# A norm's first tile made in two parts, token rows turned one tile later, 58 early U blocks and eight output buffers

## The chip, the cores and the metric

The kernel runs on one core of a Trainium2 chip, as one program. The metric is the device time of one execution in microseconds (us). The kernel before takes 4063.26 us as the median of three executions (4061.71 to 4071.17).

TensorE multiplies matrices and writes the products to PSUM; VectorE and ScalarE work element by element; GpSimd (POOL) and SyncE (SP) mostly issue transfers between the chip's memory and SBUF. Each engine runs its own instructions in a fixed order and waits for the others by semaphores.

## The reference

Two request groups, a context of 128 tokens and a latent grid of 512 tokens, go through the same weights; the kernel carries all 640 tokens side by side as columns. There are two layers. The first mixes tokens by a gated short convolution, the second by a bidirectional state-space scan (SSD). Behind each stands a PEER mixer, in which each token picks 8 x 16 of 16384 single-neuron experts:

```python
hn = rmsnorm(x, norm_mix_g[i]) * (1 + scl_a) + sh_a      # and again ahead of peer, with scl_f, sh_f
# short_conv_mixer
bg, cg, xv = jnp.split(h @ w_in, 3, axis=-1)
return (bg * dwconv3(cg * xv, conv_w, grid)) @ w_out
# peer: scores, the 16 best keys of each half, the 16 best pairs, softmax gates g, experts idx
act = jnp.einsum('td,thkd->thk', tb, u[ib])
out = jnp.einsum('thk,thkd->td', jax.nn.gelu(act, approximate=False) * gb, v[ib])
# end of the trunk
return rmsnorm(x, norm_f_g), states
```

All of it is in 32-bit floats.

## The kernel before

**Layout.** `x` lies in SBUF as 8 feature tiles of 128 partitions (features) x 640 columns (tokens, 512 latent and 128 context). A product at full accuracy is three matmuls of rounded parts: high x high, high x low, low x high (`mm3`, L128 to L130). So each operand is split: ScalarE writes the high part (L92 for weights, L123 for activations), VectorE subtracts it to get the low part (L101, L124). For weights these are `wr` (raw), `wh`, `wl`, and `ur`, `uh`, `ul` for the expert keys U.

**The norm** (`norm`) goes through the 8 feature tiles: VectorE multiplies a tile of `x` by the reciprocal root `rs` (L330), ScalarE applies scale and shift to the latent and the context columns separately (L332, 512 and 128 columns), then the tile is split into its high and low part (`chi`, `clo` in the conv layer, `shi`, `slo` in the SSD layer, `hnh`, `hnl` ahead of the experts). Ahead of the experts a function `token_rows` is called for each tile (as `keep`): POOL copies a few tokens' columns out of it into `some` (L774), TensorE transposes them (`pss`, `psx`, L776), and after four tiles ScalarE copies the rows out (`hrow`, L778).

**The conv layer** follows its norm with 24 weights: `cg`, `xv` and `bg` in turn for each of 8 output tiles. In the first output tile (`rows=(j == 0)`) the products go by feature tile, so that they can follow the norm. Transposes of `silurow` (`srow`, L436) stand near by. Products of the norm's output have 320 columns (half of 640).

**The experts.** Of the 512 latent tokens, 464 are done densely: for each of 128 blocks of 128 experts, TensorE multiplies the block of U by the tokens (`pact`, 24 matmuls of 464 columns), ScalarE applies Gelu into a ring of five buffers `ga` (L511), VectorE multiplies by the gates `gt` (L577) to get `h`, and TensorE multiplies `h` by the block of V (`acc` and `rot`, 24 matmuls more). The other 176 tokens' worth of work (48 latent tokens, and the context in 128 parts) is done by gathers: an indirect transfer of 128 rows of U and V side by side (`uv`, 1 MB, L592, issued by POOL, three buffers), a dot product (L599) and a weighted sum (L609) on VectorE. The first `NSP` blocks of U are multiplied early, while top-k and the gates run on VectorE; their `ga` is stored to memory by POOL (`adram`, L513) and read back by SP when its turn comes (`load_act`, L570). Then one loop goes over the 128 blocks of V. In its first part (block number + `LAG` below `NSP`) it has only V's products, 24 matmuls a turn; in the second part U's block three turns ahead stands beside them, 48 matmuls a turn. `GATHER` gives the gathers per turn in the two parts. VectorE adds `rot` into `sacc` (L647 the first time, L649 later).

**Order.** Most of the program is put in order by a scheduler that uses a cost model; the last part of the early blocks and the loop stand in the order in which the code is written (`manual_schedule`). Just ahead of the loop the code issues two gathers and the first `gt` on POOL's queue, then the remaining early blocks (`fill`), then three `load_act`. SP's and POOL's queues each go in order: a transfer whose buffer isn't free holds all that are behind it.

**The end.** `final` multiplies the 8 tiles by `rs` and the last norm's weight into `fo` (L218, three buffers) and stores each (`yT`, L220).

Of the kernel before, what the change touches and what calls it, by code (L numbers as in the profile page):

```python
# [9 lines left out]
F32 = mybir.dt.float32  # L10
# [5 lines left out]
AF = mybir.ActivationFunctionType  # L16
# [5 lines left out]
P = 128  # L22
NL = 512
NT = 640
# [5 lines left out]
KT = 8  # L30
D = 1024
HALF = 320
EPS = 1e-6
NBLK = 128
NSP = 56
LAG = 3
GA = 4
TB = 16
# [1 line left out]
SW = 64  # L40
CH = 5
FILL_Q = (0, 8500)
GATHER = (0.60, 1.98)
START = 4
MORE = (1, 1, 0, 4)
ADA_C = 16
# [7 lines left out]
SEGS = ((0, NL, 0), (NL, NT, 1))  # L54
# [62 lines left out]
class K:  # L117
# [28 lines left out]
    def run(s):  # L146
        nc, A = s.nc, s.A
        with ExitStack() as ctx:
# [4 lines left out]
            s.gdram = dram.tile([NBLK // GA, P, ND // SG, GA, SG], F32, name="gdram")  # L153
            s.adram = dram.tile([NSP, P, ND], F32, name="adram")
            s.sdram = dram.tile([1, 2, D], F32, name="sdram")
# [56 lines left out]
    def final(s):  # L212
        nc = s.nc
        with ExitStack() as ctx:
            tp = s.pool(ctx, "ftmp")
            for k in range(KT):
                o = tp.tile([P, NT], F32, name="fo", bufs=3)
                nc.vector.scalar_tensor_tensor(o, s.x[:, k, :], s.sv("nff", KT)[:, k:k + 1], s.rs,  # L218
                                               op0=ALU.mult, op1=ALU.mult)
                nc.sync.dma_start(s.A["yT"][:, k, :], o)  # L220
# [104 lines left out]
    def norm(s, i, j, hi, lo, tp, keep=None, ks=range(KT)):  # L325

        nc = s.nc
        for k in ks:
            t = tp.tile([P, NT], F32, name="nt", bufs=3)
            nc.vector.tensor_mul(t, s.x[:, k, :], s.rs)  # L330
            for a, b, c in SEGS:
                nc.scalar.activation(t[:, a:b], t[:, a:b], AF.Identity, bias=s.mod[i][:, 24 * j + k, c:c + 1],  # L332
                                     scale=s.gs[i][:, j, k, c:c + 1])
            s.split(hi[:, k, :], lo[:, k, :], t)
            if keep is not None:
                keep(k, t)

    def proj(s, w, hi, lo, out, rows=False):

# [144 lines left out]
    def peer(s, i):  # L484
        nc, A = s.nc, s.A
        with ExitStack() as ctx:
# [15 lines left out]
            def u_blocks():  # L502
                for a in range(NBLK):
# [7 lines left out]
                    nc.scalar.activation(g, pa, AF.Gelu)  # L511
                    if a < NSP:
                        nc.gpsimd.dma_start(s.adram[a], g)  # L513
# [7 lines left out]
            def fill(ns, steps=0):  # L521

                state["owe"] += ns
                while (steps > 0 or ns and state["owe"] > 0) and state["n"] < NSP * KT:
                    t = next(ub)
                    if not steps:
                        state["owe"] -= t
                    steps -= 1 if steps else 0
                    state["n"] += 1
                U.split(state["n"] // KT + 2)  # L530
# [8 lines left out]
            with ExitStack() as mc:  # L539
# [27 lines left out]
                def load_act(a):  # L567
                    if a < NSP:
                        t = ring.tile([P, ND], F32, name="ga")
                        nc.sync.dma_start(t, s.adram[a])  # L570
                        ga[a] = t
# [60 lines left out]
                state["owe"] = 0  # L632
                fill(0, NSP * KT - state["n"] - KT)
                for a in range(LAG):
# [16 lines left out]
                for a in range(NBLK - 2):  # L651
                    V.high(a + 2)
                    if a + LAG >= NSP:
                        U.high(a + LAG + 2)
# [21 lines left out]

                    credit += GATHER[0] if a + LAG < NSP else GATHER[1]
                    due, before = 0, slot
# [793 lines left out]
```

## Time and profile before

| what | us |
|---|---|
| runs | 4061.71, 4063.26, 4071.17 |
| profiled execution | 4057.71 |
| its span | 4056.0 |
| TensorE busy | 3915.4 (97%) |
| VectorE busy | 3394.0 (84%) |
| ScalarE busy | 1663.2 (41%) |
| POOL busy | 514.9 (13%) |
| granted TensorE clock, mean | 0.987 |

From the span's start the stages are: ada modulation, conv norm and conv layer to 277 us; the norm ahead of layer 0's experts to 304; top-k, gates and early blocks to 787; the loop to 1822; the SSD layer, whose norm stands at 1836, to 2491; the second layer's experts with their norm (2494), early blocks (to 2990) and loop (from 2999) to 4020; the last norm to 4056. "Idle before" an instruction is the time in which its engine had nothing to run, and the arrow says what ended it. The granted clock is the share of TensorE's full speed.

### The profile page before, as it was taken

How to read it: one execution, taken by the hardware profiler on the slowest of the kernel's cores; microseconds unless marked ns; L12 is line 12 of the kernel's file. 1: busy time of each engine (PE TensorE's matmuls, PEld its weight loads, DVE VectorE, ACT ScalarE, POOL GpSimd, SP SyncE). 2: the span in 40 equal slices, each digit the busy share in tenths (PEclk: the TensorE clock that was granted, in tenths of full speed). 3: DMA queues.
4: the chain of work that ended last, by engine and by line, in shares of the span. 5: the costliest groups of instructions: out<-in, count | busy, mean ns of one | idle time of the engine just before them, and what ended most of it. 6: DMA issues, size and time to landing. Idle time of an engine off the chain costs nothing.

```text
span 4056.0 us, 59421 instructions
## 1 busy us (share of the span) xinstructions
PE 3915.4 (97%) x22237; PEld 3548.9 (87%) x22237; DVE 3394.0 (84%) x6512; ACT 1663.2 (41%) x3120; POOL 514.9 (13%) x695
## 2 busy tenths in 40 slices
PE   8999999899999999999999999999989999999998
PEld 6989988788888888888899998998878888888887
DVE  8978988588878888887999856998768888888887
ACT  5233344433334333336555644334433333343333
POOL 0010000011112212211110101000011111121211
PEclk9999999999999999999999999999999999999999
DMA  6643258988889989973333234226888898998995
GB/s 228 218 154 121 83 171 248 287 318 312 329 311 338 341 325 333 339 274 126 114 102 119 88 114 173 83 99 192 251 296 314 316 334 316 337 335 329 333 333 222
DMA packets 337451, 979.15 MB, mean 241 GB/s; under 512 B 39371, under 2 KB 174795, under 8 KB 291081
## 3 DMA queue, kind: packets, MB, share of 16 engines
q1 hardware_dynamic: 146922, 508.73, 35.7%
q0 software_dynamic: 64000, 398.47, 26.4%
q10 hardware_dynamic: 126240, 68.16, 5.9%
q8 instruction: 174, 2.85, 0.3%
q14 instruction: 115, 0.94, 0.1%
HBM read 867.00 MB, written 108.14 MB: 240 GB/s over the span
## 4 chain that ended last, share of the span: by engine, by line
issue 41%; PE 29%; DVE 15%; POOL 9%; DMA 4%; ACT 2%; POOLq 0%; SPq 0%; ACTq 0%; DVEq 0%
POOL uv L592 9%; PE pact L128 2%; DMA ur<-uT 2%; PE pact L130 2%; PE pj L128 2%; PE pact L129 2%; PE pj L129 2%; PE pj L130 2%; DVE ul L101 2%; DVE wl L101 1%; PE bank L128 1%; PE bank L129 1%; PE bank L130 1%; PE bank L1189 1%; PE pg L999 1%
## 5 line engine op out<-in xcount | busy, mean ns | idle before, releaser
L128 PE MATMUL pact<-hnh,uh 128*128 128x464 f32 x2048 | 774.2, 378 | 1.0 <-DVE xt L623 1.0
L130 PE MATMUL pact<-hnh,ul 128*128 128x464 f32 x2048 | 768.3, 375 | 0.0
L129 PE MATMUL pact<-hnl,uh 128*128 128x464 f32 x2048 | 766.6, 374 | 0.0
L592 POOL DMA_INDIRECT uv<-uv,cidx x352 | 362.2, 1029 | 1698.6 <-DVE cacc L609 1567.2
L128 PE MATMUL acc<-h,wh 128*128 128x464 f32 x1536 | 575.4, 375 | 0.0
L130 PE MATMUL acc<-h,wl 128*128 128x464 f32 x1536 | 575.3, 375 | 0.0
L129 PE MATMUL acc<-h,wh 128*128 128x464 f32 x1536 | 573.1, 373 | 0.0
L92 ACT ACTIVATE wh<-wr 128x1024 fp32r<-128x1024 f32 x385 | 404.9, 1052 | 377.8 <-DMA wr<-uv 92.5
L599 DVE SCALAR_TENSOR_TENSOR uv<-uv,hrow 128x1024 f32<-128x1024 f32 x352 | 430.1, 1222 | 128.5 <-DMA uv<-uv,cidx 125.3
L101 DVE TENSOR_TENSOR wl<-wr,wh 128x1024 fp32r<-128x1024 f32 x385 | 469.8, 1220 | 54.7 <-ACT wh L92 54.4
L609 DVE SCALAR_TENSOR_TENSOR cacc<-uv,dg,cacc 128x1024 f32<-128x1024 f32 x346 | 443.4, 1282 | 0.0
L130 PEld LDWEIGHTS pact<-hnh,ul 128*128 128x128 f32 x2048 | 386.4, 189 | 45.5 <-DVE ul L101 0.3
L128 PEld LDWEIGHTS pact<-hnh,uh 128*128 128x128 f32 x2048 | 387.2, 189 | 44.6 <-DVE xt L623 1.3
L129 PEld LDWEIGHTS pact<-hnl,uh 128*128 128x128 f32 x2048 | 387.2, 189 | 44.3
L511 ACT ACTIVATE ga<-pact 128x464 f32<-128x464 f32 x256 | 141.8, 554 | 582.6 <-PE pact L130 578.9
L101 DVE TENSOR_TENSOR ul<-ur,uh 128x1024 fp32r<-128x1024 f32 x256 | 312.1, 1220 | 56.0 <-ACT uh L92 55.9
L92 ACT ACTIVATE uh<-ur 128x1024 fp32r<-128x1024 f32 x256 | 268.3, 1050 | 184.7 <-PE pact L129 81.0
L129 PEld LDWEIGHTS acc<-h,wh 128*128 128x128 f32 x1536 | 291.0, 189 | 36.0
L130 PEld LDWEIGHTS acc<-h,wl 128*128 128x128 f32 x1536 | 290.0, 189 | 34.9
L128 PEld LDWEIGHTS acc<-h,wh 128*128 128x128 f32 x1536 | 290.7, 189 | 33.8
L601 ACT ACTIVATE dg<-dg 128x1 f32<-128x1 f32 x352 | 70.6, 200 | 540.4 <-DVE uv L599 540.0
L586 DVE TENSOR_TENSOR h<-h,h 128x464 fp32r<-128x464 f32 x256 | 163.8, 640 | 127.7 <-PE rot L129 123.8
(346 smaller groups left out, 7978.1 us busy)
## 6 DMA issues: line engine op xcount, KB each, us to landing
ur<-uT SPq DMA_DIRECT2D x256, 512.0 KB
wr<-uv SPq DMA_DIRECT2D x256, 512.0 KB
gt<-gdram SPq DMA_DIRECT2D x62, 928.0 KB
gdram<-st ACTq DMA_DIRECT2D x28, 2048.0 KB
mw<-ada_wT SPq DMA_DIRECT2D x80, 512.0 KB
adram<-ga POOLq DMA_DIRECT2D x112, 232.0 KB, 4.1
ga<-adram SPq DMA_DIRECT2D x112, 232.0 KB
wr<-ssd_w SPq DMA_DIRECT2D x48, 512.0 KB
```

Source lines behind the costliest of these rows:

```text
L92: s.K.nc.scalar.activation(hi.rearrange("p a b -> p (a b)"), s.raw[s.nh], AF.Copy)
L101: s.K.nc.vector.tensor_sub(lo.rearrange("p a b -> p (a b)"), s.raw.pop(s.ns), hi.rearrange("p a b -> p (a b)").bitcast(F32))
L128: mm(out, wh, mh, start=start, stop=False)
L129: mm(out, wh, ml, start=False, stop=False)
L130: mm(out, wl, mh, start=False, stop=stop)
L511: nc.scalar.activation(g, pa, AF.Gelu)
L586: nc.vector.tensor_sub(h2, h, h1.bitcast(F32))
L592: nc.gpsimd.indirect_dma_start(out=t[:], out_offset=None, in_=A["uv"].rearrange("l e d -> (l e) d"), in_offset=bass.IndirectOffsetOnAxis(a ...
L599: nc.vector.scalar_tensor_tensor(UV[n][:, :D], UV[n][:, :D], 1.0, rows[-1], op0=ALU.mult, op1=ALU.mult, accum_out=dg[:, n:n + 1])
L601: nc.scalar.activation(dg[:, n:n + 1], dg[:, n:n + 1], AF.Gelu)
L609: nc.vector.scalar_tensor_tensor(cacc, t[:, D:], dg[:, n:n + 1], cacc, op0=ALU.mult, op1=ALU.add)
L999: nc.tensor.matmul(g[:, q, :], oh[:, t + q, :], o1[:, t + q, :], start=True, stop=False)
```

## The change

The constant `NSP` goes from 56 to 58 and the gather rates from (0.60, 1.98) to (0.62, 2.0). `fo` gets eight buffers instead of three. In `norm`, the first feature tile is multiplied, modulated and split in two parts, columns 0 to 320 and 320 to 640; the others in one part as before. `keep` (the token rows) of tile k is called after tile k+1 is made, and that of the last tile at the end. All four norms that use this function are touched: conv, SSD, and the two ahead of the experts.

```diff
-NSP = 56
+NSP = 58
...
-GATHER = (0.60, 1.98)
+GATHER = (0.62, 2.0)
...
-                o = tp.tile([P, NT], F32, name="fo", bufs=3)
+                o = tp.tile([P, NT], F32, name="fo", bufs=KT)
...
+        late = None
         for k in ks:
             t = tp.tile([P, NT], F32, name="nt", bufs=3)
-            nc.vector.tensor_mul(t, s.x[:, k, :], s.rs)
-            for a, b, c in SEGS:
-                nc.scalar.activation(t[:, a:b], t[:, a:b], AF.Identity, bias=s.mod[i][:, 24 * j + k, c:c + 1],
-                                     scale=s.gs[i][:, j, k, c:c + 1])
-            s.split(hi[:, k, :], lo[:, k, :], t)
+
+            for p, q in ((0, HALF), (HALF, NT)) if k == 0 else ((0, NT),):
+                nc.vector.tensor_mul(t[:, p:q], s.x[:, k, p:q], s.rs[:, p:q])
+                for a, b, c in SEGS:
+                    a, b = max(a, p), min(b, q)
+                    if a < b:
+                        nc.scalar.activation(t[:, a:b], t[:, a:b], AF.Identity, bias=s.mod[i][:, 24 * j + k, c:c + 1],
+                                             scale=s.gs[i][:, j, k, c:c + 1])
+                s.split(hi[:, k, p:q], lo[:, k, p:q], t[:, p:q])
             if keep is not None:
-                keep(k, t)
+                if late is not None:
+                    keep(*late)
+                late = k, t
+        if late is not None:
+            keep(*late)
```

The added lines move the code below them by nine: L330 of before is L333, L592 is L601. Where the scheduler decides, more moves than the diff says.

In the conv layer's norm, VectorE's order before has the second weight's low part (`wl` of `xv`) between the norm's tiles:

```order
L124 TENSOR_TENSOR clo<-nt,chi 128x640
L330 TENSOR_TENSOR nt<-x,rs 128x640
L101 TENSOR_TENSOR wl<-wr,wh 128x1024
L276 TENSOR_TENSOR mod_92<-mod_92,sm 128x8
L124 TENSOR_TENSOR clo<-nt,chi 128x640
L330 TENSOR_TENSOR nt<-x,rs 128x640
```

The changed program has no `wl` there, and two of them after the last tile:

```order
L333 TENSOR_TENSOR nt<-x,rs 128x640
L124 TENSOR_TENSOR clo<-nt,chi 128x640 x3
L101 TENSOR_TENSOR wl<-wr,wh 128x1024
L258 SCALAR_TENSOR_TENSOR mj,mod_92<-mw,silurow 128x1024
L101 TENSOR_TENSOR wl<-wr,wh 128x1024
```

So one weight's low part has moved from the norm's second tile to behind its last; on TensorE, the `xv` products that stood between the `cg` ones now come after them.

On TensorE, at the start of the norm ahead of layer 0's experts (`rb` belongs to the reciprocal root), before:

```order
L297 MATMUL st<-ones,sq 128x64 x5
L322 MATMUL rb<-ident,rt 128x128 x5
L776 MATMUL pss<-ident,some_2761 128x128
L776 MATMUL pss<-ident,some_2764 128x128
L776 MATMUL psx<-ident,nt 128x128
L776 MATMUL pss<-ident,some_2774 128x128
L776 MATMUL pss<-ident,some_2777 128x128
L128 MATMUL pq_2916<-hnh,wh 128x320
```

and now:

```order
L297 MATMUL st<-ones,sq 128x64 x5
L322 MATMUL rb<-ident,rt 128x128 x5
L128 MATMUL pq_2924<-hnh,wh 128x320
L785 MATMUL pss<-ident,some_2775 128x128
L785 MATMUL pss<-ident,some_2778 128x128
L785 MATMUL psx<-ident,nt 128x128
L129 MATMUL pq_2924<-hnl,wh 128x320
```

The first product of the key weights (`pq`) has moved ahead of the token rows' transposes.

On POOL, just ahead of layer 0's loop, before:

```order
L513 DMA adram<-ga 128x464 x52
L592 DMA uv<-uv,cidx 128x2048 x2
L564 DMA gt<-gdram 128x1856
L513 DMA adram<-ga 128x464 x4
L592 DMA uv<-uv,cidx 128x2048 x174
```

and now:

```order
L522 DMA adram<-ga 128x464 x52
L601 DMA uv<-uv,cidx 128x2048 x2
L573 DMA gt<-gdram 128x1856
L522 DMA adram<-ga 128x464 x6
L601 DMA uv<-uv,cidx 128x2048 x174
```

The two blocks more are stored behind the two gathers and the first `gt`, six stores there instead of four.

## Rows read from the trace of the kernel before

**Rows 1.** The page, busy time, share and instructions of each engine.

```profile
PE 3915.4 (97%) x22237; PEld 3548.9 (87%) x22237; DVE 3394.0 (84%) x6512; ACT 1663.2 (41%) x3120; POOL 514.9 (13%) x695
```

**Rows 2.** What TensorE waited for: us in total, times, longest us.

```profile
PE rot L128 <- ACT ga L511: 18.2, 2, 9.7
PE rot L128 <- DVE sacc L649: 15.8, 11, 3.9
...
PE pss L776 <- POOL some L774: 9.2, 6, 4.1
PE rot L128 <- DVE sacc L647: 6.2, 2, 3.6
...
PE bank L128 <- ACT shi L123: 4.2, 1, 4.2
```

**Rows 3.** Stretches: length, busy (count) of PE, PEld, DVE, ACT, POOL, clock, DMA share, GB/s.

```profile
64.00:277.00 213.00, 212.81 (x1453) 212.36 (x1452) 193.85 (x337) 54.67 (x69) 1.13 (x32) 1.00 0.59 195
763.00:787.00 24.00, 15.52 (x78) 13.56 (x75) 5.51 (x6) 6.70 (x10) 4.21 (x6) 0.92 0.92 291
787.00:1822.00 1035.00, 1022.86 (x4834) 909.96 (x4834) 869.50 (x1126) 385.64 (x753) 182.25 (x180) 0.99 0.88 323
1745.00:1775.00 30.00, 26.39 (x119) 23.18 (x118) 22.67 (x30) 10.04 (x23) 5.11 (x6) 0.94 0.92 355
3012.00:4020.00 1008.00, 998.63 (x4741) 889.35 (x4740) 847.10 (x1092) 377.93 (x740) 177.62 (x173) 1.00 0.89 326
```

**Rows 4.** Timeline of the conv norm: start, duration, engine, line, operation, idle before.

```profile
47.93 1.22 DVE L101 TENSOR_TENSOR wl<-wr,wh 128x1024 fp32r<-128x1024 f32 x1
...
53.45 0.83 DVE L124 TENSOR_TENSOR clo<-nt,chi 128x640 fp32r<-128x640 f32 x1
...
55.17 0.82 DVE L124 TENSOR_TENSOR clo<-nt,chi 128x640 fp32r<-128x640 f32 x1
...
60.10 0.83 DVE L124 TENSOR_TENSOR clo<-nt,chi 128x640 fp32r<-128x640 f32 x1 [0.67 <-ACT chi L123]
...
63.56 0.31 PE L128 MATMUL bg<-chi,wh 128*128 128x320 f32 x1
```

**Rows 5.** Groups by shape: count, busy us, mean ns of one, idle before.

```profile
L330 DVE TENSOR_TENSOR nt<-x,rs 128x640 f32<-128x640 f32 x32 | 26.0, 829 | 4.8 <-ACT rs L323 3.1 <-POOL some L774 0.2
L332 ACT ACTIVATE nt<-nt,mod,gs 128x512 f32<-128x512 f32 x32 | 25.8, 807 | 2.7 <-DVE nt L330 2.7
...
L332 ACT ACTIVATE nt<-nt,mod,gs 128x128 f32<-128x128 f32 x32 | 15.5, 483 | 0.0
```

**Rows 6.** Timeline of TensorE and ScalarE, norm ahead of layer 0's experts.

```profile
286.24 0.48 PE L776 MATMUL pss<-ident,some 128*128 128x128 f32 x1 [4.08 <-POOL some L774]
...
292.75 0.60 ACT L778 ACTIVATE hrow<-pss 128x512 f32<-128x512 f32 x1 [1.74 <-PE pss L776]
...
302.29 0.60 ACT L778 ACTIVATE hrow<-pss 128x512 f32<-128x512 f32 x1 [0.93 <-PE pss L776]
```

**Rows 7.** Timeline of SP and TensorE ahead of layer 0's loop, and near its end.

```profile
767.71 17.87 SPq L570 DMA_DIRECT2D ga<-adram  x3
...
778.05 0.38 PE L130 MATMUL pact<-hnh,ul 128*128 128x464 f32 x1
786.91 0.75 PE L128 MATMUL rot<-h,wh 128*128 128x464 f32 x1 [8.48 <-ACT ga L511]
...
796.54 0.67 PE L128 MATMUL rot<-h,wh 128*128 128x464 f32 x1 [3.61 <-DVE sacc L647]
...
1762.81 0.76 PE L128 MATMUL rot<-h,wh 128*128 128x464 f32 x1 [3.61 <-DVE sacc L649]
```

**Rows 8.** Chain of waits ahead of layer 0's loop: start, us, what.

```profile
774.45 10.12 DMA gt<-gdram
```

**Rows 9.** What ended VectorE's idle time before L218: us, times.

```profile
  DMA yT<-fo: 1.4, 2
```

**Rows 10.** Chain of waits near the end of layer 0's loop.

```profile
1747.27 12.49 DMA uv<-uv,cidx
```

## The prediction

> **What bounds the kernel now.** I read the busy shares first: TensorE works 97% of the span, so a microsecond counts only where TensorE is idle or where its work grows [rows 1]. Then the list of what TensorE waited for. The reader is to see there that the long waits stand in few places: twice about 9 us before the first `rot` product of a V/U loop, on `ga` of ScalarE; twice about 3 us one block later, on `sacc`; six waits in the norms before the experts, on the copies `some`; one of 4.2 us on `shi`; and eleven short ones inside the loops [rows 2]. Third, the stretches: between 64 and 277 us, and in both loops, TensorE has next to no idle time, so what is lost ahead of such a stretch is not regained in it; at 763 to 787 us it works 15.5 of 24 us [rows 3]. A product of 320 columns costs 212.81/1453 = 0.1465 us there, one of 464 columns 998.63/4741 = 0.211 us [rows 3].
>
> The sum is made against the profiled execution, 4057.71 us (span 4056.0, 1.7 us around it). The median of the runs shown, 4063.26 us, is 5.55 us above it; I move the sum's result by that.
>
> **1. The conv layer's norm: a loss of 4.2 us.** Splitting its first tile is small in itself, but it turns the scheduler's choice. Before, the second weight's low part `wl` is made at 47.93 us, between the norm's tiles, so `xv` products fill TensorE beside the `cg` ones. Now this `wl` stands behind the last `clo`, and TensorE has only `cg` during the norm: six products a tile, 6 x 0.1465 = 0.88 us, while tiles come every 55.17 - 53.45 = 1.72 us [rows 4]. All 48 `xv` products, 7.04 us, come after it. Without the 1.22 us of `wl` in between, the last `clo` should end some 1.6 us earlier than 60.93, say 59.3; then the last tile's `cg` 0.9, `xv` 7.04 and about 0.5 for the transposes of `silurow` that stand there: 67.7 against 63.56, when `bg` starts in the kernel before [rows 4]. That is +4.2, and TensorE is full up to 277 us, so it stays. Ends: +2 if early `xv` products find their `wh` sooner, +7 if the half-idle stretch lowers the clock (the granted clock was 0.94 in a stretch with 26.4 of 30 us busy [rows 3]).
>
> **2. The norms before the experts: -1.6 us each, twice.** Here TensorE stands idle 4.08 us until the copy `some` of the first whole tile, and all transposes of the token rows stand ahead of the first `pq` product [rows 6]. Now `pq` takes the first half tile, and the rows of tile k are turned after tile k+1 was made. TensorE has work some 3 us sooner, but ScalarE sets the norm's pace, so only its own gains last: a start about 0.4 us earlier (half of the tile's multiplication of 829 ns [rows 5]), its wait of 1.74 us for `pss` and the later one of 0.93 us [rows 6], 3.1 in all. Against them stand two more ScalarE instructions: 512 columns take 807 ns and 128 take 483, so 375 ns are fixed and two cost 0.75 us [rows 5]. If all waits go it is -2.3, if none goes +0.35; the order puts the transposes a tile later, where their input is old, so I take -1.6, nearer to the first. What is queued behind the later transposes on TensorE are products that had waited anyway. The end is kept: VectorE's top-k follows and starts as much earlier.
>
> The Trainium skill (VectorE: DVE Perf Modes, section "The TRN2 errata — SBUF-src ops pay a fixed extra latency per instruction") says that SBUF operations pay a fixed latency each, so that many small tiles pay it per tile and tiles of 512 or more amortize it. That speaks against halves of 320; the trace agrees with a fixed part, 375 ns [rows 5]. It is a rival below.
>
> **3. The SSD norm: -1.0 us.** The wait of 4.17 us on `shi` [rows 2] is cut for the `pj` products alone; the `bank` products of 384 columns need both halves. Between 0 and -2.
>
> **4. Two more U blocks ahead of each loop: -8.0 and -8.5 us.** The products are the same in number; 2 x 24 x 0.21 = 10.08 us of them move from the loop, where TensorE is full, to the tail ahead of it. Layer 0 before: the last early product starts at 778.05 and ends at 778.43; then 8.48 us idle until 786.91, and 3.61 us until 796.54 [rows 7]. The cause: the second of `h`'s operands, `gt`, was issued at 774.45, behind two gathers, and landed 10.12 us later [rows 8]; `rot` came 2.34 us after that, with `h`, its split and the `ga` of the last block in between. Now TensorE is busy until 788.51. What is late next is `ga`. Of the ring's five buffers, the three `ga` loads before took two that were free, and only the third waited on a store queued behind gathers and `gt` on POOL (SP was held there to 785.58 [rows 7]). With 58 blocks all three stores stand behind them, so all three loads start about 785.6; 3 x 232 KB at the 291 GB/s of this stretch [rows 3] take 2.4 us: 788.0, plus 2.34: `rot` at 790.3, an idle time of 1.8 us instead of 8.48. The second stall keeps its chain, from the `ur` load that SP issues behind those `ga` loads; I put its end at 797.8 instead of 796.54: 10.08 - 1.26 = 8.8 us gained. The two further `ur` loads of 512 KB come into the same stretch: if all of their 3.6 us (1 MB at 291 GB/s) fell on `gt`, 5.2 would be left. I take 8.0, as the gathers and `gt` are issued no later than before. Layer 1's stalls are 9.7 and 2.6 us (18.2 and 6.2 less the first ones [rows 2]); there the first idle time hides more of the two blocks: 8.5. Ends for each: 4 (the loads delay `gt`, and the second stall grows too) and 11.5 (all 10.08, and the slow clock after the long idle time goes: 0.92 was granted here [rows 3]).
>
> The Trainium skill (DMA: Bandwidth & Descriptors, section "Queues, rings and completion order") says that each DMA engine goes round between the queues that have work, a packet at a time. By that rule SP's `ur` loads take their share from POOL's `gt` at once, and the gain would stand nearer 5 than 9; the `gt` that took 10.12 us beside gathers [rows 8] fits it.
>
> **5. The gather rates.** 0.60 to 0.62 and 1.98 to 2.0 a block: the first rate holds for 55 turns of the loop instead of 53 and gives 34 gathers (55 x 0.62) instead of 31; the other 142 of 176 fall into the 71 turns at the second rate, two each. The loop moved 323 and 326 GB/s; 10 us less of 1035 make that 326 and 329, and 355 were moved at 1745 to 1775 [rows 3]. VectorE works 84% of the loop. I cost it at nothing, covered by that room; the price without the cover is the slower rival.
>
> **6. The end: -1.4 us.** With eight `fo` buffers the two waits of 1.4 us for `yT` stores go [rows 9]; the last store follows the last `fo`, so nearly all of it counts. Between -1 and -1.5.
>
> Sum: 4.2 - 3.2 - 1.0 - 8.0 - 8.5 - 1.4 = -17.9 us: 4039.8 as a profiled execution, 4045 as a median. The best ends (2 - 4.6 - 2 - 23 - 1.5) make -29, 4034; the worst (7 + 0.7 + 0 - 8 - 1) -1, 4062.
>
> **Rivals.** (a) *The cover is mostly lost*: the `ur` loads push `gt`, `ga` and the weight of the second block, and the tail gives 4 us a layer; conv loses 6; the norms give 2, the end 1.4: -5.4, about 4058. For it: a stretch with 0.92 of the DMA time used [rows 3], and SP held behind one `ga` load for 17.87 us [rows 7]. Against it: the gathers that hold POOL do not wait for these loads' buffers.
> (b) *Full cover*: 11.5 a layer, conv +2, the rest as above: -26.6, about 4037. For it: the stalls of 12.1 us are longer than the 10.08 of work. Against it: the new `ga` wait.
> (c) *Slower*: late gathers. A gather that took 12.49 us [rows 10] held `rot` 3.61 us until 1762.81 [rows 7], and 6% of clock over 30 us [rows 3] add 1.8: 5.4 us each. From 17.9/5.4 = 3.3 such events more the gain is gone; eight (four a layer) make +43 - 18 = +25, 4088. For it: three `uv` buffers, two gathers a block of 10.08 us at the end of the loop, DMA share 0.92. Against it: eleven such waits cost 15.8 us in both loops together before [rows 2], and the rate rises by 1%.
> (d) *The small halves cost what they bring*, by the fixed part: no gain in three norms and 0.75 us more in each: -17.9 + 4.2 + 2.3 = -11.4, 4052.
>
> **Chances.** The forecast, with its own range 4038 to 4051: 0.56. (a) 0.20, (b) 0.11, (c) 0.06, (d) 0.07. What a measurement can tell from no change is 0.3%, 12.2 us, so faster is below 4051. Faster: forecast and (b), 0.67; same: (a) and (d), 0.27; slower: (c), 0.06. The range runs from 4032, a little below the best ends, to 4060: it takes in (a), (b) and (d), and leaves out (c) and the last of the worst ends.
>
> **What will show it.** Right: `bg` starting near 68 us; idle before the first `rot` of each loop under 5 us, with `ga` loads, not `gt`, as what came last; second `rot` near 798; loops without more than eleven waits on `sacc`; no `yT` wait at the end. Wrong: `bg` as early as before (step 1 fails), a first `rot` after 792 (step 4), or new waits of 2 us and more on `sacc` L649's counterpart (step 5).

## The result and the profile after

The changed kernel takes 4045.37 us as the median of five runs (4035.02 to 4048.12), against 4063.26 for the kernel before; the ratio is 0.9943 (95% interval 0.9922 to 0.9963), so 15 to 32 us less. The number forecast, 4045, and its sign are met, but partly by luck. Of the terms behind it some are not met: the rates, which the prediction set to zero, carry about half of the gain when they are changed first, the norms cost time instead of coming out even, and the early blocks gave less than it said.

The profiled execution is one of 4045.37 us, span 4043.6. That is 12.4 us below the profiled span of before, which was one of the shorter runs of its kernel. TensorE, as in [rows 1], from the page:

```profile
PE 3918.1 (97%) x22237; PEld 3549.4 (88%) x22237; DVE 3394.8 (84%) x6520; ACT 1664.6 (41%) x3128; POOL 514.8 (13%) x699
```

What TensorE waited for, the counterpart of [rows 2] (us in total, times, longest; line numbers behind `norm` are nine higher):

```profile
PE rot L128 <- DVE sacc L658: 9.7, 8, 4.6
PE rot L128 <- ACT ga L520: 9.5, 2, 5.0
PE pact L631 <- DVE cacc L618: 5.8, 2, 3.1
...
PE pss L785 <- POOL some L783: 4.2, 5, 3.0
...
PE rot L128 <- DVE sacc L656: 3.7, 2, 2.5
...
PE pj L128 <- ACT shi L123: 2.6, 1, 2.6
```

The waits on `ga` have fallen from 18.2 to 9.5 us, those on `sacc` inside the loops from 15.8 in eleven to 9.7 in eight. But the wait at a change of token group (`pact` L631, L622 before) has grown from 0.4 us in one to 5.8 in two, so that both kinds together came down only from 16.2 to 15.5 in these two traces.

The conv norm, as in [rows 4], the timeline of VectorE and TensorE:

```profile
59.07 0.83 DVE L124 TENSOR_TENSOR clo<-nt,chi 128x640 fp32r<-128x640 f32 x1 [0.67 <-ACT chi L123]
60.02 1.23 DVE L101 TENSOR_TENSOR wl<-wr,wh 128x1024 fp32r<-128x1024 f32 x1
...
60.65 0.30 PE L128 MATMUL xv<-chi,wh 128*128 128x320 f32 x1
...
68.58 0.31 PE L128 MATMUL bg<-chi,wh 128*128 128x320 f32 x1
```

The last `clo` ends at 59.9 (59.3 was forecast), all `xv` products follow, and `bg` starts at 68.58 instead of 63.56. The time ahead of layer 0's loop, TensorE's timeline first and then the chain of waits (start, us, what):

```profile
801.20 0.76 PE L128 MATMUL rot<-h,wh 128*128 128x464 f32 x1 [4.54 <-ACT ga L520]
```

```profile
783.91 12.15 DMA adram<-ga
796.09 3.32 DMA ga<-adram
799.43 0.65 DVE h L586
```

In the kernel before `gt` stood in this place [rows 8], and the wait was 8.48 us [rows 7]; now a store of `ga`, issued behind the gathers and `gt`, takes 12.15 us, and its reading back 3.32 more.

One execution differs from the next by more than some of these terms. For the comparison below I therefore take two lengths out of every trace: the *tail*, from the last one-hot product (`pg`) to the first `rot` product, and the *loop*, from there to the first product of the following norm's sums. In the changed kernel the two stretches of layer 0 read so (columns as in [rows 3]):

```profile
771.17:801.20 30.03, 25.49 (x125) 22.46 (x122) 7.96 (x8) 9.87 (x14) 5.30 (x8) 0.97 0.94 309
801.20:1820.42 1019.22, 1008.76 (x4786) 898.12 (x4787) 869.19 (x1126) 384.72 (x750) 181.14 (x180) 1.00 0.89 327
```

The tail holds 25.5 us of TensorE's work in 30.0 us; in the loop 4786 products stand where the kernel before has 4834 [rows 3]. Means in us, layer 0 / layer 1:

| early blocks, rates | traces | tail | loop |
|---|---|---|---|
| 56, 0.60 and 1.98 | 3 | 23.9 / 25.5 | 1036.0 / 1033.5 |
| 56, 0.60 and 2.0 | 1 | 24.1 / 25.5 | 1035.1 / 1033.7 |
| 56, 0.62 and 1.98 | 1 | 24.7 / 24.7 | 1031.2 / 1028.9 |
| 56, 0.62 and 2.0 | 1 | 24.3 / 25.8 | 1033.1 / 1027.1 |
| 58, 0.60 and 1.98 | 1 | 31.1 / 30.6 | 1031.2 / 1036.2 |
| 58, 0.62 and 2.0 | 5 | 30.7 / 30.4 | 1018.4 / 1021.5 |

The traces are those of the kernels below; the last row leaves out the two in which the stores were moved. A row of one trace is to be read with care: the three loops of layer 1 in the first row are 1035.7, 1035.8 and 1029.1 us, with the same instructions.

### The profile page after: what moved, and what is told of

Read it like the earlier page. It is cut to its first block, busy times and chain, and to the rows that moved or that the text cites. A ratio compares the mean times of both kernels' runs of the same rounds, so it can differ in the third digit from the quotient of the medians.

```text
span 4043.6 us, 59448 instructions
## 1 busy us (share of the span) xinstructions
PE 3918.1 (97%) x22237; PEld 3549.4 (88%) x22237; DVE 3394.8 (84%) x6520; ACT 1664.6 (41%) x3128; POOL 514.8 (13%) x699
## 4 chain that ended last, share of the span: by engine, by line
issue 42%; PE 27%; DVE 15%; POOL 9%; DMA 4%; ACT 2%; POOLq 0%; SPq 0%; ACTq 0%; DVEq 0%
POOL uv L601 9%; DMA ur<-uT 2%; PE pj L129 2%; PE pj L128 2%; PE pj L130 2%; PE pact L128 2%; PE pact L130 2%; PE pact L129 2%; DVE ul L101 2%; DVE wl L101 1%; PE bank L128 1%; PE bank L129 1%; PE bank L130 1%; PE bank L1198 1%; DVE idx L819 1%
## 5 line engine op out<-in xcount | busy, mean ns | idle before, releaser
L601 POOL DMA_INDIRECT uv<-uv,cidx x352 | 362.1, 1029 | 1671.2 <-DVE cacc L618 1563.7
## 6 DMA issues: line engine op xcount, KB each, us to landing
gdram<-st ACTq DMA_DIRECT2D x28, 2048.0 KB, 11.4
```

What stands on the lines that cost most here:

```text
L601: nc.gpsimd.indirect_dma_start(out=t[:], out_offset=None, in_=A["uv"].rearrange("l e d -> (l e) d"), in_offset=bass.IndirectOffsetOnAxis(a ...
```

## The experiments

All but one were timed in five rounds or more, against the kernel before on the same chip. Differences in us are the ratio times 4060.

**Blocks and rates alone.**

```diff
-NSP = 56
+NSP = 58
-GATHER = (0.60, 1.98)
+GATHER = (0.62, 2.0)
```

> The kernel before with 58 early blocks and the gather rates 0.62 and 2.0, nothing else. By the prediction's terms (-8.0 and -8.5 in the two tails, loops unchanged): -16.5 us, about 4047. By what the two traces show between the last one-hot product and the first 50 us of each loop (-7.0 in layer 0, -4.4 in layer 1), with all differences inside the loops put down to chance: -11.4 us, about 4052. If the new rates help the loops as well (the first loop came out 4.7 us shorter than the two blocks explain): -16 to -20. First rot product of both loops after an idle time of 4 to 5 us that a ga load ends, not gt.

Measured: ratio 0.9956 (0.9943 to 0.9969), -18 us (-23 to -13). That is more than the -11.4 that I had read out of two traces; it agrees with the prediction's -16.5 and as well with the third reading, so it doesn't tell them apart. `ga` ends an idle time of 5.1 us in both layers.

**The norm alone** (the diff's part in `norm`, everything else as before).

> The kernel before with the norm alone changed (first tile in two parts, token rows a tile later). By the prediction's terms: conv +4.2, experts' norms -1.6 each, SSD norm -1.0: 0 us. By the two traces: conv +4.4, layer 0's experts' norm 0, layer 1's +0.8, SSD about -0.5: +4.7 us, about 4068. In the trace, of this kernel as of the whole change: bg starts near 68 us, VectorE's top-k of layer 0 begins 4.4 us later than before.

Measured: ratio 1.0015 (1.0006 to 1.0024), +6 us (+2 to +10). The prediction's zero is outside. `bg` starts at 69.08, top-k at 325.01 against 320.26.

**Conv norm in whole tiles.**

```diff
-            for p, q in ((0, HALF), (HALF, NT)) if k == 0 else ((0, NT),):
+            for p, q in ((0, HALF), (HALF, NT)) if k == 0 and (i or j) else ((0, NT),):
```

> The changed kernel, but the conv layer's norm makes its first tile in one part again; the other three norms keep the two parts. If the split alone turns the scheduler's order there: wl of xv back among the norm's tiles, bg near 63.6 us, and 4.4 us less than the changed kernel, about 4041 (-22 against before). If the loss at the conv layer's end has another cause, or is given back later, no change against 4045.

Measured: ratio 0.9944 (0.9930 to 0.9957), median 4038.08. `wl` is back among the norm's tiles and `bg` at 65.30 (where the norm's first `clo` comes 1.7 us later than before, too), so the split alone turns the scheduler's order. Whether the whole is faster by that the timing can't tell: the ratio equals that of the changed kernel, which was timed in another set of runs, and the median is 7 us lower.

**Eight `fo` buffers alone.**

```diff
-                o = tp.tile([P, NT], F32, name="fo", bufs=3)
+                o = tp.tile([P, NT], F32, name="fo", bufs=KT)
```

> The kernel before with eight fo buffers, nothing else, one look. By the prediction: the two waits of 1.4 us for stores gone, and the time from the first fo multiplication to the span's end 1.4 us shorter than the 11.65 us of before. Rival: the eight stores themselves take the time (320 KB each), so the last one lands when it did: no change there.

Measured, VectorE's timeline of this kernel (span 4050.6):

```profile
4040.41 6.45 DVE L218 SCALAR_TENSOR_TENSOR fo<-x,sm,rs 128x640 f32<-128x640 f32 x8 [1.54 <-ACT rs L323]
```

All eight run without a wait, and from here to the span's end it is 10.2 us instead of 11.65: -1.5. The first theory holds, by this one trace.

**Stores on ScalarE's queue.**

```diff
-                        nc.gpsimd.dma_start(s.adram[a], g)
+                        (nc.gpsimd if a < NSP - 6 else nc.scalar).dma_start(s.adram[a], g)
```

> The changed kernel, but the last six early blocks' ga is stored from ScalarE's queue instead of POOL's. If the first rot waits because these stores stand behind two gathers and gt on POOL's queue: the three ga loads no longer wait, h starts when gt lands (12.0 us after its issue in the changed kernel), and the idle time before the first rot falls from 4.5 and 5.0 us to about 1 us; some 3.5 us less per layer, 4038. If the sheer traffic of the stretch (0.93 of the DMA time) sets it: the idle time stays within 1 us of 4.5 and 5.0.

Measured: ratio 0.9944 (0.9930 to 0.9958). The idle time before `rot` did fall, to 1.34 and 1.09 us, but the tails are 32.0 and 31.4 us, longer than without this edit. The timelines of layer 0, of this kernel (last one-hot product at 768.92):

```profile
788.54 5.53 SPq L579 DMA_DIRECT2D ga<-adram  x3
798.62 1.19 DVE L586 TENSOR_TENSOR h<-ga,gt 128x464 f32<-128x464 f32 x2
800.93 0.48 PE L128 MATMUL rot<-h,wh 128*128 128x464 f32 x1 [1.34 <-ACT ga L520]
```

and of the changed one (last one-hot product at 771.17):

```profile
795.59 1.41 SPq L579 DMA_DIRECT2D ga<-adram  x3
798.54 0.64 DVE L586 TENSOR_TENSOR h<-ga,gt 128x464 f32<-128x464 f32 x1 [2.24 <-DMA ga<-adram]
```

Counted from the last one-hot product, the first `ga` load goes out 4.8 us sooner (6.1 in layer 1), but it takes 8.7 us to land instead of 2.9, and `h` starts after 29.7 us instead of 27.4 (29.1 and 28.2 in layer 1). So the fall of the idle time is not the first theory's: TensorE ends its early blocks 5.2 and 4.8 us later, and its idle time has moved ahead of that. ScalarE's timeline and TensorE's show part of it:

```profile
770.63 4.91 ACTq L522 DMA_DIRECT2D adram<-ga  x1
775.64 1.06 ACT L92 ACTIVATE uh<-ur 128x1024 fp32r<-128x1024 f32 x1 [5.42 <-issue]
...
776.75 0.48 PE L128 MATMUL pact<-hnh,uh 128*128 128x464 f32 x1 [2.51 <-ACT uh L92]
```

Issuing the first of these stores held ScalarE for 4.91 us, just behind a 2 MB store on the same queue; the next block's `uh` came late, and TensorE waited 2.51 us there. The stores no longer stand behind the gathers, and yet the loads that wait for them land no sooner. That speaks for the traffic, but ScalarE's delay is mixed into it, so this run shows neither theory.

**`gt` ahead of the gathers.**

```diff
+                load_g(0)
                 gather(0)
                 gather(1)
-                load_g(0)
```

> The changed kernel with the first gt issued ahead of the two gathers on POOL instead of behind them. If ga is what comes last (its stores still stand behind the gathers): gt lands about 5 us after its issue instead of 12, and the first rot starts no earlier, idle time 4 to 5 us as in the changed kernel, 4045. If gt is still what sets it, as in the kernel before: idle time near 0 and some 4 us less per layer, 4037.

Measured: ratio 0.9948 (0.9935 to 0.9962); the first theory holds, `ga` is what comes last. TensorE's timeline of it:

```profile
799.07 0.47 PE L128 MATMUL rot<-h,wh 128*128 128x464 f32 x1 [4.54 <-ACT ga L520]
...
3004.50 0.76 PE L128 MATMUL rot<-h,wh 128*128 128x464 f32 x1 [5.03 <-ACT ga L520]
```

The idle times are the changed kernel's, 4.54 and 5.0, with `adram<-ga` for 11.71 us and `ga<-adram` for 3.71 in the chain. `gt` is not the bound any more.

**Both rates alone.**

```diff
-GATHER = (0.60, 1.98)
+GATHER = (0.62, 2.0)
```

> The kernel before with the gather rates 0.62 and 2.0 alone (56 early blocks). By the prediction the rates cost and give nothing: loops of 1036.0 and 1033.5 us (means of three kernels with 56 blocks and the old rates) within 3 us. Rival: the rates are why layer 0's loop became 17.8 us shorter with 58 blocks where two blocks make 10.1: then this kernel's loop of layer 0 is some 5 to 7 us shorter, near 1030, and the late gather near the loop's end (a wait of 3.6 to 4.9 us on sacc) is halved.

Measured: ratio 0.9971 (0.9959 to 0.9983), -12 us (-17 to -7). The prediction's nothing fails; the rival's place (layer 0's late gather) is not where it comes from either: that wait is 5.0 us here. What TensorE waited for in this kernel, against 15.8 us in eleven waits on `sacc` [rows 2] and 0.4 in one at a change of token group:

```profile
PE rot L128 <- DVE sacc L649: 7.7, 4, 5.0
PE pact L622 <- DVE cacc L609: 3.2, 2, 1.9
```

**The second rate alone**, 0.60 and 2.0.

> The kernel before with the second gather rate at 2.0 and the first left at 0.60. The two rates together gave -11.8 us (-6.9 to -16.6). If the second rate does it (every turn of the second part then carries exactly two gathers): about -10. If the first rate does it (the first 34 gathers come earlier and the changes of token group with them): within 3 us of before, and the waits of 1 to 2 us on sacc in the middle of layer 1's loop (3154, 3392 and 3587 us before) are still there.

Measured: ratio 0.9993 (0.9981 to 1.0005), -3 us (-8 to +2): no change that is clear of the noise. The waits stay:

```profile
PE rot L128 <- DVE sacc L649: 13.5, 10, 3.8
```

**The first rate alone**, 0.62 and 1.98.

> The kernel before with the first gather rate at 0.62 and the second left at 1.98. Both rates together gave -11.8 us, the second alone -2.8 (-7.7 to +2.0). If the first does it: -7 us or more, and the wait on sacc near 931 and 3155 us (where the 16th gather changes the token group) and those some 21 us after the second change of group (1181 and 3392 us before) are gone, as with both rates. If it takes both: within 3 us of before, with some of these waits still there.

Measured: ratio 0.9975 (0.9966 to 0.9984), -10 us (-14 to -6).

```profile
PE rot L128 <- DVE sacc L649: 6.5, 3, 3.1
PE pact L622 <- DVE cacc L609: 2.7, 2, 1.8
```

It is the first rate. The waits near the first change of token group (931 and 3155 us before) are gone; a wait of 0.4 us at 945 is left. Those on `sacc` after the second change are gone too, but at that change `pact` now waits 1.0 and 1.8 us.

The number of waits differs from trace to trace: eight `fo` buffers alone, with the old rates, show six on `sacc` of 11.2 us. The loops say it better. With 56 blocks, the two loops of a trace together take 2065.8 to 2072.8 us in the four traces at 0.60, and 2060.1 and 2060.2 in the two at 0.62. Behind the first `rot` product TensorE's waits in both loops make 22.0 to 24.8 us at 0.60, and 16.6 and 18.8 at 0.62: some 5.5 of the 9 us. The rest was not taken apart.

**58 blocks with the old rates.**

```diff
-NSP = 56
+NSP = 58
```

> The kernel before with 58 early blocks and the old rates. 55 x 0.60 + 71 x 1.98 = 173.6, so the loop's last turn but one has two or three gathers left over and takes them all at once. If blocks and rates simply add (-17.9 together, -11.8 the rates): -6 us less the cost of the leftover, some 2.5 us of VectorE and a late gather for each, so -6 to +10 us. By the prediction (blocks -16.5, rates nothing): -16.5, or about -8 with the leftover.

Measured: ratio 1.0019 (1.0010 to 1.0028), +8 us (+4 to +11): slower than before. The prediction's reading, -16.5 or -8, is out. At the end of both loops TensorE stands still; from the list of its waits:

```profile
PE rot L128 <- ACT wh L92: 21.1, 2, 11.7
```

and VectorE's timeline in layer 0 meanwhile:

```profile
1801.60 1.23 DVE L599 SCALAR_TENSOR_TENSOR uv<-uv,hrow 128x1024 f32<-128x1024 f32 x1 [1.53 <-DMA uv<-uv,cidx]
...
1805.35 1.29 DVE L599 SCALAR_TENSOR_TENSOR uv<-uv,hrow 128x1024 f32<-128x1024 f32 x1 [1.31 <-DMA uv<-uv,cidx]
...
1810.62 1.22 DVE L599 SCALAR_TENSOR_TENSOR uv<-uv,hrow 128x1024 f32<-128x1024 f32 x1 [2.75 <-DMA uv<-uv,cidx]
```

TensorE's wait of 11.75 us ends at 1813.41; VectorE works off the left-over gathers one after another and waits for each transfer. From the last `pact` product to the end of the loop it is 38.8 and 35.4 us here against 23.9 and 23.2 before.

**No halves at all**, token rows a tile later, the rest as changed.

```diff
-            for p, q in ((0, HALF), (HALF, NT)) if k == 0 else ((0, NT),):
+            for p, q in ((0, NT),):
```

> The changed kernel with no tile made in two parts in any norm; the token rows still come one tile later. By the prediction the halves bring 1 us in the SSD norm and part of 1.6 us in each norm ahead of the experts: these three norms some 3 us longer than in the changed kernel, conv 4.4 shorter. By the traces so far the halves bring nothing there: from the last conv product to VectorE's first top-k instruction the time is within 0.3 us of the kernel before, and the whole is near 4040 (4.4 less than the changed kernel).

Measured: ratio 0.9946 (0.9933 to 0.9960), median 4040.45. `bg` is at 63.64. The time from the norm's sums to VectorE's first top-k instruction is 40.4 us in layer 0 (before 40.8, changed 40.7) and 36.8 in layer 1 (37.5 and 38.2): the halves show no gain ahead of the experts. In the SSD layer they bring the first product 1.6 us nearer to the norm's sums (5.3 instead of 6.9 us), but from the sums to the output projection it is 596.6 us with them and 596.4 before: given back later; where was not looked into.

**The best of them put together**: no halves, and two of the last early blocks written ahead of `gt` and the gathers.

```diff
-            for p, q in ((0, HALF), (HALF, NT)) if k == 0 else ((0, NT),):
+            for p, q in ((0, NT),):
...
+                fill(0, (NSP - 4) * KT - state["n"])
+                load_g(0)
                 gather(0)
                 gather(1)
-                load_g(0)
...
```

(The two lines that set `state` for `fill` move up with it.)

> All tiles of the norms in one part, the rest as in the changed kernel, and ahead of the loop two of the remaining early blocks are written before the first gt and the two gathers (gt first), so that their stores stand ahead of them on POOL. If the stores behind the gathers are what holds the first rot: idle before it falls from 4.5 and 5.0 us to about 1 us, layer by layer, with no new wait among the early blocks (as the stores on ScalarE's queue had), 4 us less per layer than late token rows alone (4040.45): about 4032. If the traffic sets it: idle stays at 4 to 5 us, 4040.

Measured: 4033.21 us (4026.81 to 4041.5), ratio 0.9933 (0.9919 to 0.9947), -27 us: the fastest median of all, though its interval overlaps that of the changed kernel. TensorE's timeline:

```profile
793.92 0.47 PE L128 MATMUL rot<-h,wh 128*128 128x464 f32 x1 [2.79 <-ACT ga L520]
...
802.54 0.72 PE L128 MATMUL rot<-h,wh 128*128 128x464 f32 x1 [3.94 <-DVE sacc L656]
```

The first idle time falls from 4.5 to 2.8 us (layer 1: 5.0 to 2.3), but the second grows, 3.94 instead of 1.17 (layer 1: 3.96 instead of 2.48); the four together make 13.0 us, 13.2 in the changed kernel. The first two `ga` loads are now issued early, at 779.54 and 780.04, and the second takes 12.09 us itself. So the place on the queue was only part of the wait: the first load goes out 10.5 us sooner after the last one-hot product (13.9 us instead of 24.4), and `rot` starts 1.8 us sooner (28.3 instead of 30.0).

## Why the prediction came out right, step by step

The number is right because wrong terms cancelled.

- **Conv norm (+4.2): right.** `bg` came 5.0 us later, the end of the conv layer 4.4 us (TensorE's first product of the next norm 282.86 instead of 278.44). The cause, the `wl` moved behind the last tile by the split, is shown by the kernel with whole tiles there.
- **Norms ahead of the experts (-1.6 each): too large.** Top-k starts 4.35 us later than before in layer 0, which is the conv loss without a gain of its own. Over all traces the time from the sums to top-k is 41.4 / 38.1 us with the old norm (seven kernels) and 40.3 / 37.9 with the changed one (five): -1.1 and -0.2. The step that failed is "the order puts the transposes a tile later ... so I take -1.6". (One norm in the same order differs by up to 1.5 us from trace to trace, so even -1.1 is not sure.) TensorE's wait of 4.08 us [rows 6] became one of 2.48 in the changed kernel, and its first work after it came 1.1 us sooner (289.52 less the 4.42 of the conv layer, against 286.24). But ScalarE's waits for the transposes, which were to go, stayed for the most part, and VectorE got a new one. What the two waited for in both norms, before and then in the changed kernel:

```profile
ACT hrow L778 <- PE pss L776: 4.6, 4, 1.7
```

```profile
ACT hrows L787 <- PE pss L785: 3.5, 2, 1.8
ACT hrow L787 <- PE pss L785: 2.5, 4, 1.1
DVE nt L333 <- PE psx L785: 6.5, 4, 2.3
```

  ScalarE waits 6.0 us instead of 4.6 in these two; over all traces it is 3.1 to 6.0 with the changed order and 4.6 to 6.1 with the old one, on average about 1 us less over both norms, where 2.7 us a norm were to go. The transpose `psx` reads `nt` itself, of which there are three buffers; turned a tile later, it holds its buffer longer, and VectorE waits for it before it can make a further tile. All seven traces with the changed order have this wait, 3.7 to 6.6 us; those with the old order have at most 0.3. More `nt` buffers were not tried.

  TensorE's timeline of the changed kernel, layer 0's norm ahead of the experts:

```profile
289.52 0.63 PE L128 MATMUL pq<-hnh,wh 128*128 128x320 f32 x1 [2.48 <-ACT hnh L123]
...
291.29 0.47 PE L785 MATMUL pss<-ident,some 128*128 128x128 f32 x1 [0.36 <-POOL some L783]
```

  The first `pq` product now stands ahead of the transposes, as the order said.
- **SSD norm (-1.0): no gain.** The wait on `shi` fell from 4.17 to 2.59 us, and the layer gave it back. The rival (d), no gain from the halves, is nearest to what the runs show in these three norms; its price of 0.75 us each is not shown.
- **Blocks (-8.0 and -8.5): the mechanism right, the size wrong.** The tails grew by 6.8 and 4.9 us for 10.08 of work, with `ga` instead of `gt` as what came last, as forecast; the idle time was 4.5 us where 1.8 was forecast: the first `ga` load was issued 24.4 us after the last one-hot product (795.59 and 771.17) instead of 22.6 (785.6 and 763.0), since the store took 12.15 us, and the read took 3.3 us instead of 2.4. At the new rates the two blocks shorten tail and loop by 7.5 us in layer 0 and by 1.4 in layer 1 (the kernels with 0.62 in the table: 1056.6 and 1053.3 for 56 blocks, 1049.1 and 1051.9 for 58). The timed runs say -6 for both (-18 with the rates, -12 the rates). By the prediction's own sign, a first `rot` after 792, this step failed: it starts at 801.20, or at 793.05 when the 8.15 us are taken off by which the last one-hot product was late (771.17 against 763.02).
- **Rates (0): the failed step.** "I cost it at nothing, covered by that room" looked at the mean of the traffic. The rates decide which turn of the loop each gather falls into, and that has a price of its own. The first rate alone gives -10 us, and some 5.5 of the 9 us that the traces show of it are shorter waits of TensorE in the loops. And without new rates the 58 blocks make the kernel slower, as two or three gathers are left for the loop's end (55 x 0.60 + 71 x 1.98 = 173.6 of 176). So rates and blocks don't add: the rates give 12 us with 56 blocks, and 26 with 58 (+8 against -18). The slower rival (c) had the mechanism, late gathers, and the price, about 5 us a wait, but stood on the wrong side: it was the old rates that had more of them.
- **End (-1.4): right**, -1.5.

So two errors cancelled, and that the sum came out at 4045 is luck: -10 to -12 from the rates that were not counted, and some 10 us too many in norms and blocks by the traces, 16 by the timed parts (-6 instead of -16.5, and +6 instead of 0). What stays open: the parts run alone make -18 + 6 - 1.5 = -13.5, near the -12.4 between the two traces, while the timed change is -15 to -32; the intervals of the parts and of the change are wide enough for both. Loops and the stage from the first top-k to the last one-hot product differ from trace to trace with the same instructions in the same order (442.8 to 446.6 us for that stage of layer 0), and how much of the sum that makes was not worked out. Why the rate 0.60 is worse than 0.62, gather by gather, was not settled either; at layer 0's first change of group SP issues `hrow` at 923.55 and the 928 KB of `gt` 1.3 us behind it, at 0.62 (both rates) 3.8 us behind it (920.19 and 924.00), but that this is the reason was not tried.

## What to carry to other kernels

A rate or a count that fits a loop's length belongs to the length: when the length changes, work out how many items are left for the end, and try the rate by itself, with the old length and with the new one, before crediting the other edit. Making the first tile smaller brings work sooner only if the engine that sets the pace gets it done sooner, and under an automatic scheduler it can move a weight that has nothing to do with it. Work that is put off holds the buffer of its input longer: look for who wants that buffer. Filling an idle stretch shows the next late thing: look for what stands behind the fill on the same queue, and for what shares its traffic. And when an idle time shrinks, see whether the work behind it came sooner, or the work ahead of it ended later.

## What the runs showed of the hardware

The same wait can cost the clock or not. At the end of layer 0's loop TensorE waits 2.0 to 2.1 us in thirteen of the fourteen traces, and then runs the same twenty small products and one block of `acc`. In the kernel before the granted clock of that stretch was 0.53, nearly all of it at the lower of its two levels (1.2 of 2.4 GHz); in the changed kernel it was 1.00, the upper one. Stretches of each (columns as in [rows 3]), before and after:

```profile
1823.90:1831.20 7.30, 7.26 (x31) 6.92 (x32) 1.12 (x3) 3.28 (x4) 0.00 (x0) 0.53 0.01 2
```

```profile
1820.40:1824.50 4.10, 4.08 (x31) 3.95 (x32) 1.02 (x3) 2.60 (x4) 0.00 (x0) 1.00 0.01 4
```

The same 31 products took 7.26 and 4.08 us, a difference of 3.2 us that no edit made: of the thirteen traces nine ran them at a granted clock of about 0.55, three at 0.71, and only the changed kernel at 1.00. The runs of one kernel lie up to 18 us apart. For the kernel before, the shortest of 23 took 4050.37 us with a mean granted clock of 0.987, the longest 4068.83 with 0.983. 0.004 of 4060 us is 16 us, so by this estimate most of the spread goes with the clock.
